# A new deal of the eight PSUM banks in a FoX attention layer with a SwiGLU feed-forward

## The chip, the core and the metric

The kernel runs on one core of a Trainium2 chip. The metric is the device time of one execution in microseconds (us); the time of a kernel is the median over its runs.

## What is computed

The input is a sequence of 1024 tokens of width 1024, with 16 learned meta tokens put ahead of it, so 1040 positions. The core computes one layer of forgetting attention with 16 heads of 64, then a SwiGLU feed-forward with 2816 hidden units, then a last RMS norm. Cut to what matters:

```python
hn = rms_norm(h, attn_norm)
q, k, v, gate, f_logit = split(hn @ w_in)        # 16 heads of 64
q, k = rms_norm(q, q_gain), rms_norm(k, k_gain)  # per head
c = cumsum(log_sigmoid(f_logit + b_f))           # per head, along the tokens
s = q @ k.T * 64**-0.5 + c[query] - c[key]
s = where(key_pos <= query_pos, s, -inf)
h = h + (softmax(s) @ v * sigmoid(gate)) @ w_out
hn = rms_norm(h, ffn_norm)
a, u = split(hn @ ffn_w_in)
h = rms_norm(h + (silu(a) * u) @ ffn_w_out, final_norm)[16:]
```

## The kernel before

All of it is one function. Large products are made of two reduced-precision halves of each operand (`h` and `l` at the end of a name), so that each product takes three matmuls: high by high, high by low, low by high. A half is made by a cast on ACT, and the other by a subtraction on DVE.

**Attention** works on pairs of heads, numbered 0 to 7. A pass over one pair is written as a string of steps: `steady` at L575, `before` at L576 for the pass before the last, `final` at L577. The string interleaves the attention of pair p with the preparation of pair p+1, in program order. The steps and their lines:

- `P0` to `P8`: nine projection tiles `pj_0` to `pj_8` (bank taken in `proj_unit`, matmuls L189 to L195, 16 for `pj_0` and 24 for each other). Tile 0 holds the last 16 tokens. It is evacuated by a copy on ACT (`last`, L204) and an addition on DVE (L205); the others by ACT (L209, L211) and DVE (L212, L220).
- `N`: the norms of q and k. `T`: the transposes `ptk`, `ptq` and `ptl` (L318, L337) into PSUM. Each is split into halves by ACT (L301, L304) and DVE (L302, L305) to `tk`, `tq` and `tl`, and these are put into place by DMA.
- `G`: the two gate tiles `pg_0` and `pg_1` (L445 to L447, 24 matmuls each, evacuated on DVE at L452).
- `S`: the scores of one head and one half of the queries. Each tile `S_e_j` (head e of the pair, key block j) takes two matmuls (L356, L357) and is evacuated to `sb` by ACT (L363); then POOL applies the causal mask (L368) and DVE takes the running maximum `rm` (L374, L378).
- `M`: that maximum transposed by PE (`pm`, L387), reduced by DVE, and spread by PE (`pb`, L392). `X`: subtraction on DVE (L398) and exponential on ACT (L399).
- `O`: scores times values (`O`, L410), copied out by ACT (`o`, L412). `Z`: the sums over keys (`Z`, L431). `L` and `C`: the gate is loaded and combined. `W`: the weights of the pair after the next are loaded and split (ACT L96, DVE L98).
- `A`, in the last pass alone: the output projection (L504 to L506), which accumulates into four tiles `acca` at a time (taken in `acc_tile`, L512), and later `accb`.

**The feed-forward's first product** is a seven-product scheme (Strassen-Winograd) for each of 22 hidden tiles. Each of the seven is a function call `prod` (L718), 12 matmuls into one bank named `f`. Before them the normed rows are transposed by `put` (L648; matmuls L656, split by ACT L659 and DVE L660), which takes its banks by turns from S, S, M, O. For the first three hidden tiles two products each are placed early in the program by `ffn1_early` (L730), between the transposes and the rest. **The second product** accumulates into four banks at a time (`banks`, L906).

**PSUM** has eight banks, and every tile above takes one whole bank. They are dealt in four groups by tag. In a group, each new tile of the program takes the bank that comes free first, and waits until the tile that was in it has been read:

```python
BANKS = {'m': 4, 'S': 2, 'M': 1, 'O': 1}
def bank(tag, name):
    return ps.tile([P, 512], F32, tag=tag, name=name, bufs=BANKS[tag])
```

Group m serves `pj`, `ptk`, `ptq`, `ptl`, `pg`, `acc` and `f`; group S the score tiles; group M `pm`, `pb` and `Z`; group O the tile `O`.

**The order on each engine** isn't the order of the program. A scheduler simulates the program on a time line of its own and gives every engine a fixed list; an instruction that would wait for a bank in that simulation is placed later, behind others that are ready. On the chip each engine works through its list in order: a waiting instruction holds up all that stand behind it.

Of the kernel before, what the change touches and what calls it, by code (L numbers as in the profile page):

```python
# [30 lines left out]
def f32v(ap):  # L31
    return ap.bitcast(F32)
# [3 lines left out]
def fox_block(ctx, tc, hT, hN, wqkvg, w0f, w0g, wo, w1, w2, g_attn, g_ffn, g_fin, g_q, g_k, b_f, out):  # L36
# [38 lines left out]
    sm = ctx.enter_context(tc.tile_pool(name="sm", bufs=1))  # L75
    ps = ctx.enter_context(tc.tile_pool(name="ps", bufs=2, space=PS))

    BANKS = {'m': 4, 'S': 2, 'M': 1, 'O': 1}

    def bank(tag, name):  # L80
        return ps.tile([P, 512], F32, tag=tag, name=name, bufs=BANKS[tag])

# [394 lines left out]
    def oproj(hf):  # L477

        cs = slice(512 * hf, 512 * hf + 512)
        ob = big.tile([P, NK, D], F32R, tag=("xh", "xl")[hf], name=f"ob{hf}")  # L480

        def raw_tile(name, src):
            raw = wp.tile([P, 512], F32, tag="wraw", name=name, bufs=3)
            nc.sync.dma_start(raw, src)
            return raw

        def stage_o(k):
            raw = state[k]["o", hf][0] if k == NK - 1 else raw_tile(f"ogr{hf}_{k}", ogd[k, :, cs])
            nc.scalar.copy(ob[:, k, :512], raw)
            nc.vector.tensor_tensor(ob[:, k, 512:1024], raw, f32v(ob[:, k, :512]), ALU.subtract)  # L490

        def stage_wo(dc, k):
            raw = raw_tile(f"wor{hf}_{dc}_{k}", wo[k][:, 512 * dc : 512 * dc + 512])
            hi = wp.tile([P, 512], F32R, tag="wh", name=f"woh{hf}_{dc}_{k}", bufs=8)
            lo = wp.tile([P, 512], F32R, tag="wl", name=f"wol{hf}_{dc}_{k}", bufs=8)
            nc.scalar.copy(hi, raw)
            nc.vector.tensor_tensor(lo, raw, f32v(hi), ALU.subtract)
            return hi, lo

        def mm(acc, i, k, w, whole=False):  # L500
            first = k == 0 or (k == NK - 1 and not whole)
            last = k == NK - 1 or (k == NK - 2 and not whole)
            oh, ol = ob[:, k, i * P : (i + 1) * P], ob[:, k, 512 + i * P : 512 + (i + 1) * P]
            nc.tensor.matmul(acc, lhsT=oh, rhs=w[0], start=first, stop=False)  # L504
            nc.tensor.matmul(acc, lhsT=oh, rhs=w[1], start=False, stop=False)
            last_mm[0] = nc.tensor.matmul(acc, lhsT=ol, rhs=w[0], start=False, stop=last)  # L506

        def add(dc, i, acc, src):
            ds_ = slice(512 * dc, 512 * dc + 512)
            nc.vector.tensor_tensor(h1[4 * hf + i][:, ds_], acc, src[:, ds_], ALU.add)  # L510

        def acc_tile(n, dc, i):  # L512
            return bank("m", f"acc{n}{hf}_{dc}_{i}")

        for dc in range(2 - hf):
            accs = [acc_tile("a", dc, i) for i in range(4)]
            for k in range(NK - 1):
                if dc == 0:
                    stage_o(k)
                w = stage_wo(dc, k)  # L520
                for i in range(4):
                    mm(accs[i], i, k, w, hf == 1)
                if k + 2 < NK:
                    yield
            if dc == 0:
                for i in range(4 * hf, 4 * hf + 4):
                    h1.append(ap_.tile([P, D], F32, tag="QQQQVVKK"[i], name=f"h1_{i}", bufs=4 if i < 4 else 2))
                    nc.sync.dma_start(h1[i], hN[META + i * P : META + (i + 1) * P, :])
            if hf == 0:
                for i in range(4):  # L530
                    add(dc, i, accs[i], h1[i])
            yield
        stage_o(NK - 1)
        if hf == 1:
            w = stage_wo(0, NK - 1)
            for i in range(4):
                mm(accs[i], i, NK - 1, w, True)
                add(0, i, accs[i], h1[4 + i])
            w = [stage_wo(1, k) for k in range(NK)]
        else:  # L540
            w = [stage_wo(dc, NK - 1) for dc in range(2)]
        for i in range(4):
            for dc in range(hf, 2):
                acc = acc_tile("b", dc, i)
                for k in range(NK) if hf == 1 else (NK - 1,):
                    mm(acc, i, k, w[k] if hf == 1 else w[dc], hf == 1)
                add(dc, i, acc, h1[4 * hf + i])
            nc.sync.dma_start(hd[4 * hf + i], h1[4 * hf + i])
            yield i
# [7 lines left out]
    gate0 = [[t[:, k * P : (k + 1) * P] for k in range(NK)] for t in (g0h, g0l)]  # L557
    proj_begin(0)
    n0 = 7
    pjs = [bank("mmmmSSM"[j], f"pj0_{j}") for j in range(n0)]  # L560
    for k in range(NK):
        for j in range(n0):
            proj_mm(0, j, k, pjs[j])
# [15 lines left out]
    for p in range(-1, NK):  # L579
        for op, *a in (first if p < 0 else steady if p + 2 < NK else before if p + 1 < NK else final).split():  # L580
            a = [int(x) for x in a]
# [129 lines left out]
    def split(src, name):  # L711
# [3 lines left out]
        nc.vector.tensor_tensor(lo, src, f32v(hi), ALU.subtract)  # L715
        return hi, lo

    def prod(t, n, s, op):  # L718
        pp = bank("m", f"f{n}_{t}")
        for k in range(4):  # L720
            ks = slice(k * P, (k + 1) * P)
            bh, bl = RB[op](k)
            nc.tensor.matmul(pp, lhsT=s[0][:, ks], rhs=bh, start=(k == 0), stop=False)  # L723
            nc.tensor.matmul(pp, lhsT=s[0][:, ks], rhs=bl, start=False, stop=False)  # L724
            nc.tensor.matmul(pp, lhsT=s[1][:, ks], rhs=bh, start=False, stop=(k == 3))  # L725
        return pp
# [3 lines left out]
    def ffn1_early(t):  # L730

        x1, c11 = (t512("cmb", f"wa{t}_{c}") for c in range(2))
        for c, r in enumerate((x1, c11)):
            nc.sync.dma_start(r, w1[t, 0, :, 512 * c : 512 * c + 512])
        p1 = prod(t, 1, split(x1, f"a11_{t}"), "b11")
        nc.scalar.copy(x1, p1)
        p2 = prod(t, 2, split(c11, f"a12_{t}"), "b21")
        tt(c11, p2, x1, ALU.add)
        return x1, c11
# [10 lines left out]
    def ffn1(t, raw, early):  # L750
# [10 lines left out]
        if early is None:  # L761
            p1 = prod(t, 1, w, "b11")
            x1 = t512("cmb", f"x1_{t}")
            nc.scalar.copy(x1, p1)
        else:
            x1, c11 = early
# [137 lines left out]
    nprod = [0]  # L904

    def banks(name):  # L906
        nprod[0] += 1
        tags = ("SSMO", "mmmm")[nprod[0] % 2]
        return [bank(g, f"y{name}_{n}") for n, g in enumerate(tags)]

    def left(name, h):
# [10 lines left out]
    def prod2(name, n, blocks, upto=NHP, ahead=None, after=None):  # L922
        py = banks(n)
        for h in range(upto):
            g = left(name, h)
            if ahead is not None:
                ahead(h)
            w = split(blocks[h], f"w{n}_{h}")
            for i in range(4):
                mm(py[i], i, h, g, w)  # L930
            if after is not None:
                after(h)
        return py
# [165 lines left out]
```

## Time and profile before

| | |
|---|---|
| median of 3 runs | 1472.07 us (1471.94 to 1474.59) |
| the profiled execution | 1471.29 us, span 1469.6 us |
| PE busy in the span | 1395.4 us, 95% |
| DVE, ACT, POOL busy | 1032.4 us (70%), 675.3 us (46%), 453.2 us (31%) |
| mean granted TensorE clock | 0.979 of full speed |
| matmuls | 6699 |

PE is the engine that runs matmuls, PEld its loading of weights, DVE the vector engine, ACT the scalar engine, POOL the general engine, SP the one that issues DMAs. A row of a timeline gives the start, the duration, the engine and line, what was written from what, and in brackets how long the engine stood idle before it and whose work ended that. A number such as 0.50 under PEclk is the TensorE clock granted in that stretch, as a share of full speed (2.4 GHz), so 0.50 is the lower level, 1.2 GHz. The profiled execution took 1.7 us more than the span, which lies around it. Matmuls overlap each other, so the time from start to start says what one costs.

### The profile page before, as it was taken

What the parts mean: (1) busy time and instruction counts of PE and PEld (TensorE: products, weight loads), DVE (VectorE), ACT (ScalarE), POOL (GpSimd) and SP (SyncE); (2) the same over time, 40 slices, a digit from 0 to 9 for tenths busy, and PEclk for the clock granted to TensorE, in tenths of its full rate; (3) what the DMA queues carried; (4) which work ended last, traced back from release to release, by engine and by line L of the source; (5) the groups of instructions that cost most, each with busy time, mean ns of one, the idle gap of its engine ahead of it and who ended that gap; (6) DMA issues with size and microseconds to landing.
All of it is one profiled execution on the core that took longest, in us unless ns stands there. A gap on an engine that the chain in (4) does not pass through costs nothing. (4 is left out here: it accounts for less than half of the span.)

```text
span 1469.6 us, 20413 instructions
## 1 busy us (share of the span) xinstructions
PE 1395.4 (95%) x6699; PEld 1123.5 (76%) x6699; DVE 1032.4 (70%) x1819; ACT 675.3 (46%) x1444; POOL 453.2 (31%) x532
## 2 busy tenths in 40 slices
PE   7999898999999898999799999999999999999996
PEld 7897777878878777756468788888888888876874
DVE  7647566757757666667887786666666666799696
ACT  6445445555555545555654433223332323434535
POOL 4002524324252525334224011111111111496082
PEclk9999999999999999999899999999999999999998
DMA  6334234250614233175463233333323227653343
GB/s 197 108 98 133 73 95 114 52 165 23 168 46 133 72 109 97 30 176 181 170 229 115 100 108 108 107 108 107 107 94 107 89 91 271 233 171 98 94 143 144
DMA packets 103197, 178.86 MB, mean 122 GB/s; under 512 B 16553, under 2 KB 25778, under 8 KB 103090
## 3 DMA queue, kind: packets, MB, share of 16 engines
q1 hardware_dynamic: 103090, 177.55, 38.9%
q8 instruction: 53, 0.87, 0.2%
q14 instruction: 54, 0.44, 0.1%
HBM read 109.46 MB, written 38.54 MB: 101 GB/s over the span
## 5 line engine op out<-in xcount | busy, mean ns | idle before, releaser
L193 PE MATMUL pj<-wh,xhb 128*128 128x384 f32 (+1 forms) x512 | 181.2, 355 | 15.6 <-DVE last L205 10.2
L368 POOL TENSOR_SCALAR_AFFINE_SELECT sb<-sb 128x128 f32<-128x128 f32 (+2 forms) x160 | 60.4, 380 | 431.5 <-ACT sb L363 430.8
L194 PE MATMUL pj<-wl,xhb 128*128 128x384 f32 (+1 forms) x512 | 179.5, 351 | 0.0
L195 PE MATMUL pj<-wh,xlb 128*128 128x384 f32 (+1 forms) x512 | 177.2, 350 | 0.0
L363 ACT ACTIVATE sb<-S,nb 128x512 f32<-128x512 f32 (+4 forms) x224 | 118.2, 537 | 126.2 <-PE S L357 124.3
L422 POOL TENSOR_TENSOR t<-t,sb 128x512 f32<-128x512 f32 (+4 forms) x160 | 139.5, 898 | 0.0
L802 POOL TENSOR_TENSOR gs<-u,u 128x512 f32<-128x512 f32 x11 | 14.2, 1287 | 380.4 <-DVE u L789 380.4
L193 PEld LDWEIGHTS pj<-wh,xhb 128*128 128x128 f32 x512 | 100.4, 196 | 20.2 <-DVE last L205 11.5
L378 DVE TENSOR_TENSOR rm<-rm,sb 128x512 f32<-128x512 f32 (+4 forms) x160 | 85.1, 532 | 38.1 <-POOL sb L368 18.1
L398 DVE TENSOR_TENSOR sb<-sb,pb 128x512 f32<-128x512 f32 (+4 forms) x224 | 95.7, 496 | 21.8 <-PE pb L392 21.8
L194 PEld LDWEIGHTS pj<-wl,xhb 128*128 128x128 f32 x512 | 100.6, 196 | 4.1 <-issue 2.4
L195 PEld LDWEIGHTS pj<-wh,xlb 128*128 128x128 f32 x512 | 100.1, 196 | 3.8 <-issue 2.4
L399 ACT ACTIVATE sb<-sb 128x512 f32<-128x512 f32 (+4 forms) x224 | 93.6, 476 | 11.7 <-DVE sb L398 8.3
L410 PE MATMUL O<-sb,V 128*64 128x512 f32 (+4 forms) x448 | 94.4, 471 | 2.9 <-ACT sb L399 2.9
L356 PE MATMUL S<-Q,K 128*128 128x512 f32 (+4 forms) x224 | 80.8, 361 | 16.2 <-ACT sb L363 16.2
L357 PE MATMUL S<-Q,K 128*128 128x512 f32 (+4 forms) x224 | 72.3, 325 | 0.8 <-DMA Q<-tq 0.8
L356 PEld LDWEIGHTS S<-Q,K 128*128 128x128 f32 (+1 forms) x224 | 39.0, 174 | 44.0 <-ACT sb L363 28.0
L410 PEld LDWEIGHTS O<-sb,V 128*64 128x64 f32 (+1 forms) x448 | 35.4, 137 | 42.4 <-issue 22.2
L769 DVE TENSOR_TENSOR u<-f,x 128x512 f32<-128x512 f32 x19 | 13.1, 692 | 64.7 <-PE f L725 64.6
L96 ACT CAST wh<-wraw 128x512 fp32r<-128x512 f32 (+1 forms) x64 | 38.2, 606 | 40.1 <-DMA wraw<-wqkvg 31.6
L374 DVE TENSOR_TENSOR rm<-sb,sb 128x400 f32<-128x400 f32 (+1 forms) x32 | 20.5, 642 | 49.6 <-ACT sb L363 49.5
L98 DVE TENSOR_TENSOR wl<-wraw,wh 128x512 fp32r<-128x512 f32 x56 | 40.1, 736 | 12.2 <-ACT wh L96 12.2
(1374 smaller groups left out, 3940.6 us busy)
## 6 DMA issues: line engine op xcount, KB each, us to landing
Q<-tq SPq DMA_DIRECT2D x128, 128.0 KB, 2.3
wraw<-wqkvg SPq DMA_DIRECT2D x56, 256.0 KB, 3.6
av<-w SPq DMA_DIRECT2D x22, 512.0 KB, 3.2
gs<-qs SPq DMA_DIRECT2D x44, 256.0 KB, 2.6
ga<-qa SPq DMA_DIRECT2D x33, 256.0 KB, 2.9
K<-tk SPq DMA_DIRECT2D x64, 128.0 KB, 2.4
wor<-wo SPq DMA_DIRECT2D x32, 256.0 KB, 3.0
a11r<-w SPq DMA_DIRECT2D x22, 256.0 KB, 3.2
```

The lines of the kernel that those rows point to most:

```text
L193: nc.tensor.matmul(o, lhsT=xh[k][:, sl], rhs=wh, start=(k == 0), stop=False)
L194: nc.tensor.matmul(o, lhsT=xh[k][:, sl], rhs=wl, start=False, stop=False)
L195: last_mm[0] = nc.tensor.matmul(o, lhsT=xl[k][:, sl], rhs=wh, start=False, stop=(k == NK - 1))
L356: nc.tensor.matmul(psx[:n, s0:], lhsT=kk[:, j * P : j * P + n], rhs=q[:, 0, s0:], start=True, stop=False)
L357: nc.tensor.matmul(psx[:n, s0:], lhsT=kk[:, j * P : j * P + n], rhs=q[:, 1, s0:], start=False, stop=True)
L363: nc.scalar.activation(sj, psx[:n, s:], AF.Identity, bias=nbias[c][:n, j, head : head + 1], scale=1.0)
L368: nc.gpsimd.affine_select(out=sj[:, : t_end - s], in_=sj[:, : t_end - s], compare_op=ALU.is_ge, fill=NEG, base=b + s - j * P, pattern=[[1, ...
L378: nc.vector.tensor_tensor(rm[:n, s:], rm[:n, s:], sj, ALU.max)
L398: nc.vector.tensor_tensor(sj, sj, mx[:n, s:], ALU.subtract)
L399: nc.scalar.activation(sj, sj, AF.Exp, bias=0.0, scale=1.0)
L410: nc.tensor.matmul(po[r, s:], lhsT=st["V"][:n, j, r], rhs=sj, start=(i == 0), stop=(i == nt - 1))
L422: nc.gpsimd.tensor_tensor(total[e][:n, s:], src[:n, s:], sj, ALU.add)
```

## The change

Group m gives one bank to group S. The fourth of the tiles `acca` and one of the first seven `pj` of the start move to S with it. The `f` tiles of the first feed-forward product are no longer all in group m: a counter takes them through all eight banks. The second product's groups of four are made up anew. No operation is added or taken away; lines behind L717 stand three further down.

```diff
-    BANKS = {'m': 4, 'S': 2, 'M': 1, 'O': 1}
+    BANKS = {'m': 3, 'S': 3, 'M': 1, 'O': 1}
...
         def acc_tile(n, dc, i):
-            return bank("m", f"acc{n}{hf}_{dc}_{i}")
+            return bank("mmmS"[i] if n == "a" else "m", f"acc{n}{hf}_{dc}_{i}")
...
-    pjs = [bank("mmmmSSM"[j], f"pj0_{j}") for j in range(n0)]
+    pjs = [bank("mmmSSSM"[j], f"pj0_{j}") for j in range(n0)]
...
+    nprod1 = [0]
+
     def prod(t, n, s, op):
-        pp = bank("m", f"f{n}_{t}")
+        nprod1[0] += 1
+        pp = bank("mSMmSOmS"[nprod1[0] % 8], f"f{n}_{t}")
...
     def banks(name):
         nprod[0] += 1
-        tags = ("SSMO", "mmmm")[nprod[0] % 2]
+        tags = ("SSSO", "mmmM")[nprod[0] % 2]
```

What this does to the scheduler's lists is seen in three places. In the names, the first numbers are the tile's own, as above, and the last is a running number that tells tiles of different passes apart.

**The end of the third pass (pair 2), on PE.** Before, the last product `O_1` is followed at once by score tiles of the next pair and then by a projection:

```order
L410 MATMUL O_1_3523<-sb_1_8_3214,V_1862 64x16
L356 MATMUL S_0_1_3680<-Q_1_0_3370,K_1_3342 128x400
L357 MATMUL S_0_1_3680<-Q_1_0_3370,K_1_3342 128x400
L356 MATMUL S_0_2_3688<-Q_1_0_3370,K_1_3342 128x272
L357 MATMUL S_0_2_3688<-Q_1_0_3370,K_1_3342 128x272
L193 MATMUL pj_4_3948<-wh_0_3564,xhb 128x384
```

Now transposes, a projection's beginning and the smaller score tiles of the other half stand there:

```order
L410 MATMUL O_1_3523<-sb_1_8_3214,V_1862 64x16
L318 MATMUL ptq_1_3623<-ident,raw_2_2789 128x128 x2
L318 MATMUL ptq_1_3623<-ident,raw_3_2790 128x128 x2
L189 MATMUL pj_0_3725<-wh_0_3564,xtail 128x256
L190 MATMUL pj_0_3725<-wl_0_3565,xtail 128x256
L189 MATMUL pj_0_3725<-wh_1_3570,xtail 128x256
L356 MATMUL S_0_3_3444<-Q_0_0_3365,K_0_3341 128x256
L357 MATMUL S_0_3_3444<-Q_0_0_3365,K_0_3341 128x256
L356 MATMUL S_0_4_3452<-Q_0_0_3365,K_0_3341 16x16
```

The score tiles that stood right behind `O_1` moved later, and `pj_4` with them.

**The same place on ACT.** Before, the copy of `O_1` stands ahead of the two evacuations of score tiles:

```order
L412 COPY o_1_3542<-O_1_3523 128x512
L363 ACTIVATE sb_0_0_3423<-S_0_0_3420,nb_253 128x512
L363 ACTIVATE sb_0_0_3675<-S_0_0_3672,nb_253 128x512
L460 ACTIVATE Ga_1_3644<-cg_1_3642 128x512
L204 COPY last_3742<-pj_0_3725 16x256
```

Now:

```order
L363 ACTIVATE sb_0_1_3431<-S_0_1_3428,nb_253 128x400
L363 ACTIVATE sb_0_2_3439<-S_0_2_3436,nb_253 128x272
L96 CAST wh_5_3594<-wraw_5_3592 128x512
L412 COPY o_1_3542<-O_1_3523 128x512
L301 ACTIVATE tq_1_0_3628<-ptq_1_3623,gqk 128x512
L363 ACTIVATE sb_0_3_3447<-S_0_3_3444,nb_253 128x144
L363 ACTIVATE sb_0_4_3455<-S_0_4_3452,nb_253 16x16
L96 CAST wh_6_3600<-wraw_6_3598 128x512
L363 ACTIVATE sb_0_0_3423<-S_0_0_3420,nb_253 128x512
L96 CAST wh_7_3606<-wraw_7_3604 128x512
```

Two evacuations moved ahead of the copy, and that of `S_0_0` behind it and behind one of three weight casts.

**The gate of the third pass, on PE.** Before, `ptk_0` stands eight rows ahead of this piece, and score and `O` matmuls follow until `pg_0` begins:

```order
L356 MATMUL S_1_7_2994<-Q_0_1_2702,K_0_2411 128x256
L357 MATMUL S_1_7_2994<-Q_0_1_2702,K_0_2411 128x256
L410 MATMUL O_0_3103<-sb_0_0_2745,V_1862 64x512
...
L387 MATMUL pm_0_1_3128<-ident,rm_1_2949 128x128
...
L410 MATMUL O_0_3103<-sb_0_4_2525,V_1862 64x16
L445 MATMUL pg_0_3465<-xhb,wh_0_2634 128x512
```

Now:

```order
L318 MATMUL ptk_0_3343<-ident,raw_0_2787 128x128 x2
L318 MATMUL ptk_0_3343<-ident,raw_1_2788 128x128 x2
L410 MATMUL O_1_3523<-sb_1_0_2953,V_1862 64x512
L431 MATMUL Z_0_3326<-t_0_0_3116,one 64x512
L431 MATMUL Z_0_3326<-t_0_1_3117,one 64x512
L318 MATMUL ptq_0_3356<-ident,raw_0_2787 128x128 x2
L318 MATMUL ptq_0_3356<-ident,raw_1_2788 128x128 x2
L337 MATMUL ptl_3375<-ident,raw_3_2791 128x16
L445 MATMUL pg_0_3465<-xhb,wh_0_2634 128x512
```

Between `ptk_0` and `pg_0` there are now three large matmuls and the small transposes.

**The entry of the feed-forward, on PE.** Before, an early product (`f_11`, hidden tile 11) runs among the transposes:

```order
L725 MATMUL f_11_8930<-b_2_8078,a_11l 128x512
...
L723 MATMUL f_11_8930<-b_3_8079,a_11h 128x512
L724 MATMUL f_11_8930<-b_7_8083,a_11h 128x512
L656 MATMUL ptt_2_8724<-ident,hl_0_8697 128x128 x4
L656 MATMUL ptb_0_8802<-ident,h_4_8436 128x128 x2
L656 MATMUL ptt_2_8731<-ident,t_2_8719 128x128 x4
```

Now the transposes follow each other, and the first early product in a bank that they use comes behind the last of them:

```order
L656 MATMUL ptb_3_8867<-ident,h_7_8442 128x128 x4
L656 MATMUL ptt_3_8851<-ident,t_3_8796 128x128 x4
L656 MATMUL ptt_3_8874<-ident,h_7_8442 128x128 x4
L726 MATMUL f_0_8890<-b_0_8076,a_0h 128x512
L727 MATMUL f_0_8890<-b_4_8080,a_0h 128x512
```

Of the six early products, the two in group m still stand ahead of the transposes, and the other four behind.

## Rows read from the trace of the kernel before

**Rows 1.** Stretches: start:end, length, PE PEld DVE ACT POOL busy, PEclk, DMA, GB/s.

```profile
164.00:247.00 83.00, 79.02 (x421) 64.71 (x421) 55.10 (x115) 44.97 (x104) 29.64 (x47) 0.96 0.36 96
765.00:830.00 65.00, 62.39 (x298) 50.80 (x297) 49.54 (x98) 31.50 (x79) 17.34 (x12) 0.93 0.31 108
830.00:1245.00 415.00, 415.00 (x1785) 335.37 (x1785) 279.01 (x431) 127.48 (x218) 57.44 (x44) 1.00 0.34 115
```

**Rows 2.** The waits of PE: waiter, releaser, us in total, times, longest.

```profile
PE S L356 <- ACT sb L363: 16.2, 22, 2.0
PE pj L193 <- DVE last L205: 10.2, 6, 1.8
PE ptq L318 <- DVE tk L305: 1.9, 1, 1.9
```

**Rows 3.** Timeline, end of the third pass: PE, ACT, DVE; last, PE in the fourth.

```profile
331.18 0.45 PE L356 MATMUL S<-Q,K 128*128 128x400 f32 x1 [1.30 <-ACT sb L363]
333.96 0.69 PE L193 MATMUL pj<-wh,xhb 128*128 128x384 f32 x1 [1.68 <-DVE last L205]
...
329.95 0.58 ACT L412 COPY o<-O 128x512 f32<-128x512 f32 x1 [3.75 <-PE O L410]
330.44 1.27 ACT L363 ACTIVATE sb<-S,nb 128x512 f32<-128x512 f32 x2
332.25 0.36 ACT L204 COPY last<-pj 16x256 f32<-16x256 f32 x1
...
333.49 0.41 DVE L205 TENSOR_TENSOR last<-pj,last 16x256 f32<-16x256 f32 x1
...
412.70 0.45 PE L356 MATMUL S<-Q,K 128*128 128x400 f32 x1 [0.63 <-ACT sb L363]
```

**Rows 4.** Stretches behind the first and the second such place, columns as in rows 1.

```profile
166.40:173.20 6.80, 5.28 (x16) 5.28 (x17) 6.80 (x13) 3.78 (x11) 6.80 (x6) 0.51 0.01 4
251.90:255.30 3.40, 3.40 (x13) 3.40 (x12) 3.40 (x7) 1.98 (x7) 3.40 (x3) 0.50 0.00 0
255.30:258.70 3.40, 3.40 (x23) 3.37 (x22) 2.89 (x9) 0.76 (x3) 3.40 (x4) 1.00 0.12 30
```

**Rows 5.** Timeline of PE in the middle of the feed-forward's first product.

```profile
1005.08 0.39 PE L723 MATMUL f<-bb,s_5h 128*128 128x512 f32 x1
1005.31 0.40 PE L724 MATMUL f<-bb,s_5h 128*128 128x512 f32 x1
```

**Rows 6.** The page's costliest groups: xcount, busy us, mean ns, idle before.

```profile
L96 ACT CAST wh<-wraw 128x512 fp32r<-128x512 f32 (+1 forms) x64 | 38.2, 606 | 40.1 <-DMA wraw<-wqkvg 31.6
```

**Rows 7.** Timeline, PE and DVE: both windows of `ptk` in the third pass, and `Z`.

```profile
281.19 0.60 PE L318 MATMUL ptk<-ident,raw 128*128 128x128 f32 x4
284.87 0.68 DVE L305 TENSOR_TENSOR tk<-ptk,tk 128x512 fp32r<-128x512 f32 x1
299.92 0.60 PE L318 MATMUL ptk<-ident,raw 128*128 128x128 f32 x4
303.70 4.19 DVE L398 TENSOR_TENSOR sb<-sb,pb 128x512 f32<-128x512 f32 x9
309.02 0.67 DVE L305 TENSOR_TENSOR tk<-ptk,tk 128x512 fp32r<-128x512 f32 x1
308.03 1.08 PE L431 MATMUL Z<-t,one 128*64 128x512 f32 x4
```

**Rows 8.** Timeline of PE in the last pass of attention.

```profile
718.92 0.30 PE L387 MATMUL pm<-ident,rm 128*128 128x128 f32 x1 [2.39 <-ACT woh L496]
763.86 0.79 PE L504 MATMUL acca<-woh,ob 128*128 128x512 f32 x1 [2.26 <-ACT ob L489]
```

**Rows 9.** The feed-forward's entry: PE, DVE, and a stretch with the columns of rows 1.

```profile
818.72 0.79 PE L723 MATMUL f<-bb,s_0h 128*128 128x512 f32 x1 [2.19 <-ACT bb L659]
...
818.15 0.68 DVE L715 TENSOR_TENSOR s_0l<-s,s_0h 128x512 fp32r<-128x512 f32 x1
...
818.50:825.30 6.80, 6.17 (x15) 4.41 (x16) 4.60 (x9) 4.99 (x9) 0.00 (x0) 0.50 0.46 154
```

## The prediction

> **What bounds the kernel now.** I first read the busy times by stretch. In the middle of the feed-forward's first product PE is busy for all of 415.00 us at full clock; in the attention's first full pass it lacks four of 83 us and its clock is at 0.96; at the feed-forward's entry it is at 0.93 [rows 1]. So PE's list sets the time, and only its idle pieces and its stretches at the lower clock can be won. Next I read the waits of PE: the two lines that come back in every pass are scores that wait for ACT's evacuation, 16.2 us in 22 waits, and projections that wait for DVE's `last`, 10.2 us in 6 [rows 2]. The timeline of the third pass shows where these two meet. PE ends `O_1`, wants a bank of group S, and stands idle for 1.30 us, because the evacuation that frees it stands on ACT behind the copy of `O_1`, which could only start at 329.95. Then `pj_4` waits 1.68 us more for a bank that `pj_0` holds until DVE has read it, at 333.90; DVE waited for ACT's copy at 332.25, and that stood behind the same evacuations [rows 3]. After this pause the clock falls to 0.50 for 3.40 us, in which 13 matmuls are done, where the next 3.40 us hold 23 [rows 4].
>
> The place comes six times, from 163 to 577 us. Five of the six score waits are of 1.30 as the one shown, one is of 0.63, 7.1 together, and the six projection waits are the whole 10.2 [rows 2, 3]. The clock falls each time: for two such stretches of 3.40 in the first place and for one in each other, so seven stretches [rows 4].
>
> **The change, part by part.** All is set against the profiled execution, 1471.29 us, which lies 0.8 below the median of the runs.
>
> *The feed-forward through eight banks.* Its matmuls already follow each other every 0.23 us [rows 5] without a gap [rows 1]. A bank that comes free earlier has nobody waiting for it: 0. A rule of the Trainium skill speaks for more: "Perfetto Trace Analysis", section "Matmul Optimizations", asks that all eight banks be leveraged. By it the product itself would be faster; by the row it can't be, since four banks leave PE no idle time to give back. The measured row decides, and the rule goes to the rivals.
>
> *End of a pass.* With three S banks the list puts `ptq`, `pj_0` and small scores behind `O_1`. Two score evacuations stand ahead of the copy, so two banks are free when PE arrives, and PE has transposes and a projection to go on with. The two waits and the pause go, and with them the falls of the clock. Gain: 7.1 + 10.2 = 17.3 for the waits, and for each slow stretch ten matmuls of 3.40 / 23 = 0.148, so 1.5, times seven, 10.4 [rows 4]. Together **-27.7**. What is late next is ACT: copy 0.58, one score evacuation of 0.64 (half of the two in [rows 3]) and two casts of 0.61 [rows 6] are 2.4 us until the bank of `S_0_0` is free. Some 26 projection matmuls stand on PE ahead of the next tile that needs it, at 0.148 each 3.8 us, so I take this as covered; without that cover the 1.30 is back, and with the pause the clock's fall (second rival).
>
> *The gate of each pass.* This is the new wait. With three m banks `pg_0` takes the bank of `ptk_0`, and must wait for `tk` on DVE. Before, the low half ended at 285.55, which is 3.76 after `ptk` had ended at 281.79, and eight rows of other work lay between [rows 7]. Now one `O` matmul, two of `Z` and the `ptq` transposes do: about 0.5, 1.0 and 0.5, some 2 us by [rows 7] (`Z` 1.08 in all, `ptk` 0.60). So the wait is 1.8 if the split takes as long as it did there, and 0 if ACT and DVE take it up at once. I take 1.4, near the first end: the same two queues are as full, and the one case in which something waited for such a split cost 1.9 [rows 2]. Seven gated passes: +10 (0 to 13). Where that pause is longest the clock may fall too; two of seven at 1.5: **+13** in all. `pg_1` takes `ptq`'s bank, but 21 matmuls of `pg_0` stand ahead of it, 4.9 us by the pitch of [rows 5]: 0. Behind the waiting `pg_0` on PE stands `pm` of the next half; it is not due earlier than it was.
>
> *The other score waits* are 16.2 - 7.1 = 9.1 in 16. A third bank lets PE run one tile further ahead of ACT. It takes between none and all; where ACT itself is the slower it only puts the wait off, so I take a third: **-3** (0 to -9).
>
> *The last pass.* `acca`'s fourth tile takes a bank of S, so its 21 matmuls are moved between the scores and `pm`, or to the end. They are 4.9 us of work without a wait of their own. The wait ahead of `pm`, 2.39 with smaller ones behind it, and the one ahead of `acca` at 763.86, 2.26 [rows 8], can be filled. I take 3 for the first place, and 2 and a slow stretch's 1.5 for the last: **-6.5** (0 to -8).
>
> *The feed-forward's entry.* Of the six early products four now stand behind the transposes. Their 48 matmuls, 11.2 us at 0.233 [rows 5], no longer lie between transposes that wait for ACT and DVE. In exchange some nine DVE operations of 0.68 [rows 9], which made these products' operands and read them, are no longer in the transposes' way: 6.1 won back. That leaves **+5** (0 to +11). What was lost there before, a wait of 2.19 and a stretch of 6.8 us with 15 matmuls [rows 9], stays in one form or another.
>
> *The start* has three banks instead of four for the first transposes and the gate: **+1** (0 to +3). The second product's banks only change owners between groups of four: 0.
>
> Sum: -27.7 + 13 - 3 - 6.5 + 5 + 1 = -18.2, so **1453.1 us**.
>
> **The rivals.** *The gate becomes the bound (slower).* The third pass's second window shows a split that ended at 309.69, 9.2 after its `ptk` at 300.52 [rows 7]. If `tk` stands as late for the gate, each pass waits 9.2 - 2 = 7.2, 50 in all instead of 10, and all seven clocks fall, 10.4 instead of 3: +48, so 1501. It decides from about 3.3 a pass: to end 2.9 above the time before, 21.1 must be lost again; five more falls of the clock are 7.5 of it, and the rest is 1.9 a pass on top of my 1.4. For it: DVE's list decides, and DVE is the second busiest [rows 1]. Against it: ahead of that split DVE had the exponentials' nine subtractions to do, 4.19 us in one piece [rows 7]; in the changed list only small maxima and evacuations stand there. Chance 0.11. The skill has a rule that speaks for this case: "TensorE: Matmul & The Clock Gate", section "A second HAM failure mode: psum-queue depth-cycling", tells of a kernel in which cycling through PSUM banks left small idle pieces between groups of matmuls, and the clock swung. The trace agrees that small pieces are enough, with 1.30 and 1.68 ahead of a fall [rows 3, 4]; that dealing banks in turn makes them, no row shows.
>
> *The stop at the end of a pass is only displaced (slower).* The freeing of `S_0_0`'s bank stands behind the copy of `O_1` and two weight casts, and a cast waits for its DMA. If that lands late, PE stands at the next scores as it did before, and the clock falls as before. Then the -27.7 are gone and the rest stays: 1480.8. It decides once the evacuation is more than 3.8 us behind PE's arrival. Against it: the casts before came without being waited for at this place. Chance 0.10.
>
> *The gate's wait is hidden (faster still).* If the split is taken up at once, the 13 go: 1440. Chance 0.14.
>
> *All eight banks make the first product itself faster.* Then what could be won is what the stretch ahead of the middle lacks, 65.00 - 62.39 = 2.6 of idle time and about 3.3 of slow clock (29 matmuls of 0.233 fit in 6.8, 15 were done [rows 1, 9]), and my +5 falls away: about 1442. Chance 0.02.
>
> *Most of it cancels.* The list changes as shown but half of the gain at the end of a pass is lost to the same clock at the gate: 1467 to 1474. Chance 0.07.
>
> **How the numbers follow.** The forecast's chance is 0.56, with its own range from 1444 to 1465. A measurement of this kernel can tell some 0.2% from no change, 2.9 us. Faster by more: forecast, hidden gate and eight banks, 0.56 + 0.14 + 0.02 = 0.72. Within it: 0.07. Slower: 0.11 + 0.10 = 0.21. The range takes in the hidden gate with the other terms' better ends, down to 1434, and the cancelled and part of the displaced case up to 1478; it leaves out the long gate and some of the displaced stop, 0.2 together.
>
> **What would show it.** Right: no wait of PE for `last` (L205) at the end of a pass, score waits of 6 us or so in all, at most two or three stretches at 0.50 in the attention, a wait of `pg` (L445) for `tk` of 1 to 2 us in seven places, and the middle of the first product at its 0.23 as before. Wrong: waits of `pg` of more than 4, a score wait behind the casts at each pass's end, or an entry of the feed-forward that is longer by more than 11.

## The result, and the profile after

The changed kernel took 1450.01 us (median of four runs, 1445.11 to 1452.52), the kernel before 1473.33 beside it: a ratio of 0.9835, with a 95% interval from 0.9803 to 0.9866. The forecast was 1453.1, with a range from 1434 to 1478. The profiled execution took 1449.52 us against 1471.29, 21.8 less.

The sum was nearly right, and several of its terms were not. What follows is about both.

The head of the page, with the busy times of the engines:

```profile
span 1447.9 us, 20369 instructions
PE 1381.0 (95%) x6699; PEld 1115.0 (77%) x6699; DVE 1041.0 (72%) x1819; ACT 679.2 (47%) x1444; POOL 448.4 (31%) x532
```

The stretches that answer to [rows 1], with the same columns:

```profile
164.00:247.00 83.00, 80.98 (x455) 66.49 (x454) 60.09 (x128) 49.01 (x115) 34.76 (x58) 1.00 0.34 98
765.00:830.00 65.00, 58.12 (x277) 46.66 (x275) 51.58 (x92) 28.60 (x61) 12.94 (x8) 0.97 0.27 93
830.00:1245.00 415.00, 415.00 (x1788) 336.22 (x1787) 276.61 (x420) 131.45 (x224) 65.54 (x49) 1.00 0.36 126
```

Between 164 and 247 us, in the attention, PE does 455 matmuls where it did 421, and the clock is at 1.00 instead of 0.96. In the middle of the feed-forward's first product nothing changed: 415.00 of 415.00 busy, 1788 matmuls and 1785 before. (The middle row is not the same work as in [rows 1]: the kernel is some 20 us further there.)

The waits of PE, to be laid beside [rows 2]:

```profile
PE acca L505 <- DVE wol L497: 7.3, 2, 6.8
...
PE pm L387 <- DVE rm L376: 5.7, 5, 2.0
PE accb L504 <- DVE h L510: 5.0, 2, 3.5
PE pj L190 <- DVE wl L98: 5.0, 2, 2.6
...
PE S L356 <- ACT sb L363: 0.6, 2, 0.4
```

Scores waited 16.2 us and now wait 0.6; the line of `last` (10.2 in 6) is gone. No line of `pg` has appeared. Grown are waits for what DVE makes: `wol` and `wl` (the low halves of weights), 0.2 and 0.3 us in the kernel before, `rm` (the running maximum), of which only L378 was waited for (2.7, now 2.2), and the addition `h` at L510, which was not waited for.

The end of the third pass. PE, then ACT:

```profile
303.72 0.86 PE L410 MATMUL O<-sb,V 128*64 128x272 f32 x7
304.51 0.66 PE L318 MATMUL ptq<-ident,raw 128*128 128x128 f32 x4
304.92 0.36 PE L189 MATMUL pj<-wh,xtail 128*128 128x256 f32 x1
...
304.74 0.59 ACT L412 COPY o<-O 128x512 f32<-128x512 f32 x1
305.21 0.71 ACT L301 ACTIVATE tq<-ptq,gqk 128x512 fp32r<-128x512 f32 x1
```

PE goes from `O_1` into the transposes and a projection without a bracket, so without idle time, while ACT makes the copy. That is the pause of [rows 3] gone. And with it the clock: of the seven slow stretches that lay behind the six places, none is left between 85 and 630 us.

To see where the 21.4 us between the two lists of matmuls lie, I gave each matmul the time that its shape usually takes from start to start in the kernel before (1310.0 us in all, the same for both kernels). What a kernel takes beyond that is its loss, and the losses can be compared over the same amount of work, also where the order differs:

| PE's work, us | place | loss before | loss after | difference | forecast |
|---|---|---|---|---|---|
| 0 to 80 | start | 12.6 | 14.7 | +2.1 | +1 |
| 80 to 530 | six passes | 72.8 | 46.1 | -26.7 | -17.7 |
| 530 to 640 | last passes | 28.2 | 31.2 | +3.0 | -6.5 |
| 640 to 740 | feed-forward's entry | 12.7 | 12.9 | +0.2 | +5 |
| 740 to the end | both products | 13.6 | 13.6 | 0.0 | 0 |

The six passes gave more than forecast and the last passes less; these errors nearly cancelled.

The usual times decide to which row a loss at a boundary goes, so the table is firm in its sum and less so in its rows: with other usual times from the same trace the six passes come to between -24 and -31, and the rows of the last passes and the entry move against each other. Two places need no usual times, because both kernels have done the same matmuls there, shape by shape: after 3893 and after 4025 matmuls, on either side of the first product's beginning. PE, first in the kernel before, then in the changed one:

```profile
798.99 0.39 PE L724 MATMUL f<-b,a_0h 128*128 128x512 f32 x1
828.90 0.40 PE L723 MATMUL f<-bc,s_0h 128*128 128x512 f32 x1
```

```profile
773.59 0.48 PE L727 MATMUL f<-b,a_1h 128*128 128x512 f32 x1
807.40 0.39 PE L728 MATMUL f<-bb,s_0l 128*128 128x512 f32 x1
```

The changed kernel is 25.4 us ahead at the first and 21.5 at the second, and 21.5 it stays. So the entry cost 3.9 and not 0.2: in the table, the wait of 2.26 at 763.86 [rows 8] and the slow clock behind it, which belong to the last pass of the kernel before, fall into the entry's row. By the same count the changed kernel is 1.9 behind after 351 matmuls (79.58 against 77.68), and 28.6 ahead after 3271 (618.78 against 647.41), just before the output projection begins in both. So the passes up to there gave 30.5, and the last pass lost 3.2.

### The profile page after: what moved, and what is told of

Read it like the earlier page. It is cut to its first block, busy times and chain, and to the rows that moved or that the text cites. A ratio compares the mean times of both kernels' runs of the same rounds, so it can differ in the third digit from the quotient of the medians.

```text
span 1447.9 us, 20369 instructions
## 1 busy us (share of the span) xinstructions
PE 1381.0 (95%) x6699; PEld 1115.0 (77%) x6699; DVE 1041.0 (72%) x1819; ACT 679.2 (47%) x1444; POOL 448.4 (31%) x532
## 4 chain that ended last, share of the span: by engine, by line
PE 72%; DVE 13%; DMA 7%; issue 4%; ACT 2%; SPq 1%; POOL 0%; DVEq 0%; ACTq 0%; POOLq 0%
PE f L726 10%; PE f L728 10%; PE f L727 10%; PE pj L193 5%; PE pj L194 5%; PE pj L195 5%; DMA wraw<-wqkvg 5%; PE O L410 3%; PE y L922 2%; PE y L923 2%; PE y L921 2%; PE S L356 2%; PE S L357 2%; PE pg L445 1%; PE pg L446 1%
## 5 line engine op out<-in xcount | busy, mean ns | idle before, releaser
L193 PE MATMUL pj<-wh,xhb 128*128 128x384 f32 (+1 forms) x512 | 176.2, 346 | 7.2 <-ACT xhb L139 5.9
L194 PE MATMUL pj<-wl,xhb 128*128 128x384 f32 (+1 forms) x512 | 175.7, 343 | 0.0
L195 PE MATMUL pj<-wh,xlb 128*128 128x384 f32 (+1 forms) x512 | 172.5, 341 | 0.0
L399 ACT ACTIVATE sb<-sb 128x512 f32<-128x512 f32 (+4 forms) x224 | 94.1, 478 | 40.7 <-DVE sb L398 40.6
L193 PEld LDWEIGHTS pj<-wh,xhb 128*128 128x128 f32 x512 | 97.5, 191 | 11.4 <-ACT xhb L139 6.4
L378 DVE TENSOR_TENSOR rm<-rm,sb 128x512 f32<-128x512 f32 (+4 forms) x160 | 87.0, 544 | 20.4 <-ACT sb L363 8.6
L194 PEld LDWEIGHTS pj<-wl,xhb 128*128 128x128 f32 x512 | 97.7, 191 | 4.2 <-issue 2.4
L195 PEld LDWEIGHTS pj<-wh,xlb 128*128 128x128 f32 x512 | 97.1, 190 | 1.5
L356 PE MATMUL S<-Q,K 128*128 128x512 f32 (+4 forms) x224 | 76.2, 344 | 0.7 <-ACT sb L363 0.6
L357 PE MATMUL S<-Q,K 128*128 128x512 f32 (+4 forms) x224 | 71.3, 323 | 0.0
L98 DVE TENSOR_TENSOR wl<-wraw,wh 128x512 fp32r<-128x512 f32 x56 | 48.9, 884 | 30.7 <-ACT wh L96 30.3
L374 DVE TENSOR_TENSOR rm<-sb,sb 128x400 f32<-128x400 f32 (+1 forms) x32 | 36.8, 1150 | 24.4 <-ACT sb L363 21.3
```

What stands on the lines that cost most here:

```text
L193: nc.tensor.matmul(o, lhsT=xh[k][:, sl], rhs=wh, start=(k == 0), stop=False)
L194: nc.tensor.matmul(o, lhsT=xh[k][:, sl], rhs=wl, start=False, stop=False)
L195: last_mm[0] = nc.tensor.matmul(o, lhsT=xl[k][:, sl], rhs=wh, start=False, stop=(k == NK - 1))
L356: nc.tensor.matmul(psx[:n, s0:], lhsT=kk[:, j * P : j * P + n], rhs=q[:, 0, s0:], start=True, stop=False)
L357: nc.tensor.matmul(psx[:n, s0:], lhsT=kk[:, j * P : j * P + n], rhs=q[:, 1, s0:], start=False, stop=True)
```

## The experiments

The theory after the result: the gain is the third bank of group S, the turn of the `f` tiles through eight banks is a loss if anything, and what now holds PE up is DVE standing still beside POOL. Every run is compared with the kernel before on the same chip.

**One part of the change alone: the attention's banks.**

```diff
-        pp = bank("mSMmSOmS"[nprod1[0] % 8], f"f{n}_{t}")
+        pp = bank("m", f"f{n}_{t}")
```

> Three S and three m banks as in the change, but the feed-forward's first products all in group m as before. Theory (the gain is the end of each attention pass: score waits, waits for `last`, and the clock's falls behind them): the six passes are those of the changed kernel, so 1446 to 1455 us; score waits of PE under 2 us, none for `last`; the middle of the first product stays at 0.233 us a matmul with three banks. Rival (the products' eight banks carry part of the gain): 1460 or more, and idle time of PE inside the first product.

Measured: 1445.64 us, ratio 0.9814 (0.9785 to 0.9843). All of the gain is there without the eight banks. With three banks instead of eight the first product is as dense as before:

```profile
830.00:1245.00 415.00, 415.00 (x1789) 335.89 (x1788) 276.17 (x417) 133.31 (x227) 67.63 (x51) 1.00 0.37 127
```

The score waits are 2.3 us in 4, a little over the 2 expected.

**The other part alone: the products' turn through the banks, on the kernel before.**

> The banks stay dealt as before (four m, two S), and only the first products go through all groups in turn. Theory: the attention's seven slow-clock stretches and the 16.2 + 10.2 us of waits stay, the first product gains nothing, and the entry of the feed-forward costs up to 5 more: 1468 to 1479 us. Rival (eight banks help the product): 1462 or less.

Measured: 1475.7 us, ratio 1.0013 (1.0000 to 1.0026). No gain. Its waits in the attention are the ones of before:

```profile
PE S L356 <- ACT sb L363: 16.9, 24, 1.7
PE pj L193 <- DVE last L205: 10.2, 6, 1.8
```

By the account of losses its entry into the feed-forward (640 to 740 of the work) lost 17.2, against 12.7 before. In e1 that piece lost 7.0, in the changed kernel 12.9. So the turn costs some 4.5 to 5.9 us there. Counted by the same matmuls, e1 is 23.4 us ahead of the kernel before after 3893 and 25.8 after 4025: the attention's banks alone win 2.4 there, and this is how the changed kernel comes out with 3.9.

**The early products alone back in group m.**

```diff
-        pp = bank("mSMmSOmS"[nprod1[0] % 8], f"f{n}_{t}")
+        pp = bank("m" if nprod1[0] <= 6 else "mSMmSOmS"[nprod1[0] % 8], f"f{n}_{t}")
```

> The changed kernel, but the six early products all in group m, the later ones through all banks. By the prediction's entry term they stand among the transposes again and win back 5 us: 1445. By the changed kernel's trace, in which the entry lost nothing in all, 1447 to 1453.

Measured: 1456.25 us, ratio 0.9864 (0.9829 to 0.9899), above both expectations. The entry did get better, to a loss of 9.8. But two passes of the attention, which this edit doesn't touch in the source, lost 10.3 and 13.0 where the changed kernel lost 7.1 and 8.1. In the second of them PE waits 6.3 us at once for `rm`; I come back to that wait. This run can't tell the term by its total.

**One bank further: two m, four S.**

```diff
-    BANKS = {'m': 3, 'S': 3, 'M': 1, 'O': 1}
+    BANKS = {'m': 2, 'S': 4, 'M': 1, 'O': 1}
...
-            return bank("mmmS"[i] if n == "a" else "m", f"acc{n}{hf}_{dc}_{i}")
+            return bank("mmSS"[i] if n == "a" else "m", f"acc{n}{hf}_{dc}_{i}")
...
-    pjs = [bank("mmmSSSM"[j], f"pj0_{j}") for j in range(n0)]
+    pjs = [bank("mmSSSSM"[j], f"pj0_{j}") for j in range(n0)]
...
-        tags = ("SSSO", "mmmM")[nprod[0] % 2]
+        tags = ("SSSS", "mmMO")[nprod[0] % 2]
```

> The change taken one bank further: two m banks, four S banks (the output projection's four tiles in m, m, S, S; the second product's groups remade). Theory: score waits are down to 0.6 us in the changed kernel, so a fourth S bank wins under 1 us; two m banks make each projection wait for the evacuation of the one before the last, and the two gate tiles for both transposes' splits, 2 to 5 us a pass with falls of the clock: 1465 to 1490. Rival (more S banks still gain, m banks are plentiful): 1450 or less.

Measured: 1514.43 us, ratio 1.0269 (1.0229 to 1.0309): the direction was right, the size too small. Here PE waits again and again for the transposes' splits (`tk` and `tq`, 19.1 us in the three lines below `wl`); the largest line, though, is the low half of a weight, `wl`:

```profile
PE pj L190 <- DVE wl L98: 27.9, 6, 8.5
PE pj L189 <- DVE tk L305: 7.7, 7, 2.4
...
PE pj L193 <- DVE tq L302: 6.2, 7, 1.6
PE ptl L337 <- DVE tk L305: 5.2, 8, 0.7
```

**The bank given to group M instead of S.**

```diff
-    BANKS = {'m': 3, 'S': 3, 'M': 1, 'O': 1}
+    BANKS = {'m': 3, 'S': 2, 'M': 2, 'O': 1}
...
-    pjs = [bank("mmmSSSM"[j], f"pj0_{j}") for j in range(n0)]
+    pjs = [bank("mmmSSMM"[j], f"pj0_{j}") for j in range(n0)]
...
-        tags = ("SSSO", "mmmM")[nprod[0] % 2]
+        tags = ("SSMO", "mmmM")[nprod[0] % 2]
```

> As e1_attn_only, but the bank that group m gives up goes to group M (pm, pb, Z) instead of S: three m, two S, two M. Theory (the gain needs the third S bank): score waits stay near 16 us, the waits for `last` and some seven slow-clock stretches stay too, 1465 to 1485. Rival (any other deal makes the scheduler's list better, and S is not the point): 1455 or less.

Measured: 1483.73 us, ratio 1.0063 (1.0043 to 1.0083). The same bank taken from m gains nothing here; only as a third S bank does it make a gain. What this run loses against the kernel before it loses late: after 3305 matmuls it is 3.2 us behind, after 3751, with most of the output projection done, 17.3. There the fourth of the tiles `acca` takes one of only two S banks; that this is the cause is not shown. The pattern of before is all there, with ten stretches of 3.4 us at 0.50 behind the six places:

```profile
PE S L356 <- ACT sb L363: 14.4, 17, 1.3
PE pj L193 <- DVE last L205: 10.6, 6, 1.8
```

**What holds PE up now.** The largest single wait of the changed kernel is in the last pass. PE, DVE and POOL there, in that order:

```profile
636.32 0.80 PE L505 MATMUL acca<-wol,ob 128*128 128x512 f32 x1 [6.85 <-DVE wol L497]
...
626.85 8.27 DVE L374 TENSOR_TENSOR rm<-sb,sb 128x400 f32<-128x400 f32 x1
635.22 0.44 DVE L378 TENSOR_TENSOR rm<-rm,sb 128x272 f32<-128x272 f32 x1
635.58 0.69 DVE L497 TENSOR_TENSOR wol<-wor,woh 128x512 fp32r<-128x512 f32 x1
...
626.33 0.72 POOL L368 TENSOR_SCALAR_AFFINE_SELECT sb<-sb 128x112 f32<-128x112 f32 x1
627.03 7.65 POOL L422 TENSOR_TENSOR t<-t,sb 128x512 f32<-128x512 f32 x7
```

One maximum of two score tiles runs for 8.27 us on DVE, and ends when POOL's chain of seven additions has ended (627.03 + 7.65 = 634.68). `wol`, for which PE waits, stands behind it in DVE's list. All executions of that operation (L374), shortest, median and longest in ns, first in the kernel before, then in the changed one:

```profile
L374 DVE TENSOR_TENSOR rm<-sb,sb x32: 555/686/717, 84.2 to 704.1; 128x400 f32<-128x400 f32 x16, 128x512 f32<-128x512 f32 x16
```

```profile
L374 DVE TENSOR_TENSOR rm<-sb,sb x32: 555/743/8270, 82.6 to 680.2; 128x400 f32<-128x400 f32 x16, 128x512 f32<-128x512 f32 x16
```

The same amount of data, so the 8.27 is no work. The Trainium skill names such a thing ("SBUF — State Buffer", section "SBUF: two separate sides"): a DVE operation with two inputs in SBUF and a POOL operation that reads SBUF share a pair of ports, the one that starts first has it for its whole instruction, and the other stands. The row agrees as far as DVE stood; that it stood for a whole chain of seven, and not for one instruction, is more than the page says.

The wait inside the passes is of the same kind. At the end of the third pass, DVE and then POOL:

```profile
311.41 3.22 DVE L98 TENSOR_TENSOR wl<-wraw,wh 128x512 fp32r<-128x512 f32 x1
...
311.60 2.48 POOL L422 TENSOR_TENSOR t<-t,sb 128x512 f32<-128x512 f32 x2
```

A subtraction of 0.69 takes 3.22, and `pj_0` waits for it for 2.44 us (312.25 to 314.69). If standing beside POOL is the cause, less work on POOL at these places should help, although it comes on top of a DVE that is busier than POOL.

**The additions before the last pass on DVE.** In `attn_out`, for pair 6 and the second half of the queries (the same computation on another engine):

```diff
-                nc.gpsimd.tensor_tensor(total[e][:n, s:], src[:n, s:], sj, ALU.add)
+                eng.tensor_tensor(total[e][:n, s:], src[:n, s:], sj, ALU.add)
...
+            eng = nc.vector if (p, c) == (NK - 2, 1) else nc.gpsimd
```

> As e1_attn_only, but the 16 additions of the sums over keys (L422) of the last pair but one, second half, run on DVE instead of POOL. Theory (in the last pass a two-input DVE operation stands still beside POOL's chain of additions: 8.27 us at 626.85 in the changed kernel where such a one takes 0.64, and PE waits 6.8 for what is queued behind it): that wait goes, the 16 additions cost DVE some 8 us of its own, 1 to 7 us faster than e1: 1439 to 1445. Rival (DVE is simply full there): the wait stays or grows, 1446 to 1454.

Measured: 1447.58 us, ratio 0.9810 (0.9759 to 0.9862), no different from e1, and as a time in the rival's range. The rival's sign is not there, though: the wait of 6.8 for `wol` is gone, the longest L374 takes 1.67, and the piece from 530 to 590 of the work lost 9.6 instead of 14.5, as the theory had it. But two passes further up now each had this on DVE, with chains of POOL beside it, and lost 12.8 and 13.7. In the second of them PE waits 6.27 us at once for `rm`, and the clock is at 0.50 behind it (DVE, PE, and a stretch with the columns of [rows 1]):

```profile
475.37 9.84 DVE L378 TENSOR_TENSOR rm<-rm,sb 128x272 f32<-128x272 f32 x3
...
485.38 1.11 PE L387 MATMUL pm<-ident,rm 128*128 128x128 f32 x4 [6.27 <-DVE rm L376]
...
487.70:491.10 3.40, 3.40 (x13) 3.40 (x11) 0.81 (x2) 0.26 (x1) 1.47 (x3) 0.50 0.08 19
```

In e1 and e3 one pass had such a group of maxima, here and in e8 two, in the changed kernel none. Which passes fall into it changes with edits elsewhere; why it strikes one pass and not the next stays open.

**Half of the additions on DVE in every pass.** The same edit with the condition `(c, e) == (1, 1)`.

> As e1_attn_only, but in every pass the additions of the second head, second half of the queries, run on DVE instead of POOL (64 additions, some 30 us more for DVE in all). Theory of the stand-still beside POOL: POOL's chains at the end of the passes are half as long, single DVE operations over 1.5 us become rare, and the waits for `rm` and `wl` (9 to 11 us in e1 and the changed kernel) shrink: 1435 to 1446. Rival (DVE's own load decides): 1447 to 1465.

Measured: 1439.77 us, ratio 0.9766 (0.9727 to 0.9805). The time is in the theory's range, though the interval overlaps e1's, and DVE has 64 additions more without being the limit. But one of the theory's signs failed. The waits for `rm` were to shrink and grew, first in e1, then here:

```profile
PE pm L387 <- DVE rm L376: 9.1, 4, 5.4
```

```profile
PE pm L387 <- DVE rm L376: 14.7, 7, 2.8
```

The longest is half as long, and there are more of them. By the count of same matmuls this run is still 2.0 us behind e1 after 3251 matmuls, before the output projection begins, and 5.2 ahead after 3893: what it wins, it wins in the last pass, where the waits for `wol` and for `h` have gone.

**All additions of the second head on DVE**, with the condition `e == 1`.

> As e7, but the second head's additions of both halves run on DVE (96 additions). If POOL's chains still hold DVE up elsewhere: 1432 to 1439. If DVE's own load is now the limit: 1441 to 1455.

Measured: 1434.29 us, ratio 0.9717 (0.9678 to 0.9756), the fastest of all, 1.2 points below the changed kernel's ratio. The longest execution of the operation from above takes 1.66 us, about what it takes in e6 and e7, where it took 8.27 in the changed kernel; in the six passes PE waits 7.9 us for `rm` and `wl`, against 10.7 in the changed kernel:

```profile
L374 DVE TENSOR_TENSOR rm<-sb,sb x32: 551/670/1658, 83.9 to 667.0; 128x400 f32<-128x400 f32 x16, 128x512 f32<-128x512 f32 x16
```

The six passes (80 to 530) lost 40.7 in it, 46.1 in the changed kernel and 47.8 in e1. This run's interval lies below e1's without overlap.

**The same edit of e7 on the banks of before, and on the changed kernel.**

> The kernel before with e7's edit alone (additions of the second head, second half of the queries, on DVE), banks dealt as before. Theory (POOL's chain holds DVE up where it matters only once PE no longer stops at the end of a pass): the score waits, the waits for `last` and the slow clock stay, and the edit is worth under 6 us: 1468 to 1478. Rival (the chains on POOL cost the same under either deal): 1462 to 1467 or less.

Measured: 1461.73 us, ratio 0.9902 (0.9870 to 0.9933). The theory missed this one: it allowed 6 us and the edit brought about 14 by the ratio (the two traced executions differ by 8.9). What it said of the six passes holds. The slow stretches stay, and the waits move from one line to the other instead of going, 25.0 us against 26.4:

```profile
PE pj L193 <- DVE last L205: 21.3, 6, 3.8
...
PE S L356 <- ACT sb L363: 3.7, 8, 1.3
```

The six passes lost 69.1 instead of 72.8. More of the gain came from the last passes and the entry together (36.0 instead of 40.9), as the rival has it: POOL's chains cost something under either deal.

> The changed kernel with e7's edit. If the first products' eight banks cost the 4 to 6 us at the feed-forward's entry that e1 and the changed kernel differ by there, this lies as much above e7: 1443 to 1447. If that difference was chance: 1437 to 1442.

Measured: 1443.8 us, ratio 0.9793 (0.9745 to 0.9841). It lost 11.8 at the entry (640 to 740), e7 5.1. With e1 against the changed kernel (7.0 and 12.9) and the kernel before against e2 (12.7 and 17.2) that makes three pairs with the same sign and 4.5 to 6.7 us each (4.5 to 6.8 by the count of same matmuls). The intervals of the totals overlap in e1's and e7's pairs, so it is the piece of the trace, not the totals, that shows it.

**A try at the waits of `accb`**, with tags from m and S by turns for these tiles:

```diff
-            return bank("mmmS"[i] if n == "a" else "m", f"acc{n}{hf}_{dc}_{i}")
+            return bank("mmmS"[i] if n == "a" else "mSmS"[i], f"acc{n}{hf}_{dc}_{i}")
```

> As e1_attn_only, but the output projection's later tiles `accb` take their banks from m and S by turns instead of m alone. If the waits of `accb` for DVE's addition (5.1 us in 2) are for a bank, they go: 1440 to 1446. If they come from DVE's place in the list, no change: 1444 to 1449.

Measured: 1462.72 us, ratio 0.9931 (0.9909 to 0.9953), above both expectations. The waits of `accb` left the list, so they were for a bank; but the feed-forward's transposes take S banks at the same time, and their list was remade so that they wait for POOL:

```profile
PE ptt L656 <- POOL hl L694: 12.6, 3, 6.1
```

## Why the prediction was right, and where it wasn't

*The end of a pass (-27.7)* was right: both waits and all seven slow stretches went, and e5, without the third S bank, has both again. The waits that went are 7.1 + 10.2; the clock's share stays the price of ten matmuls in each stretch, since no run changed the clock alone.

*The gate (+13)* is the step that failed. With three m banks `pg_0` comes right behind the three transposes, as forecast, but no wait appeared. I carried the split's delay of 3.76 us over from the list before [rows 7]. The changed list in the third pass, PE and then DVE:

```profile
281.19 0.60 PE L318 MATMUL ptk<-ident,raw 128*128 128x128 f32 x4
...
284.16 0.23 PE L337 MATMUL ptl<-ident,raw 16*128 16x16 f32 x1
284.32 0.50 PE L445 MATMUL pg<-xhb,wh 128*128 128x512 f32 x1
...
283.49 0.67 DVE L305 TENSOR_TENSOR tk<-ptk,tk 128x512 fp32r<-128x512 f32 x1
```

The low half ends at 284.16, 2.38 after `ptk`, and `pg` begins at 284.32. The delay is 1.77 to 2.71 in the seven gated passes, and the work between is 2.53 here where I had 2.0. The gate's own rival (0.11) was the further off; "the wait is hidden" (0.14) was the mechanism that came, though not with its time of 1440. Scarce m banks do cost what the step was about once there are only two: 19.1 us of such waits in e4.

*The other score waits (-3)*: all but 0.6 of 9.1 went, -8.5. Of this 4.8 lay in the six passes and the rest behind them.

*What the forecast did not have* are the new waits for `rm` and `wl`, 10.7 us in the six passes. So these passes come to -27.7 - 4.8 + 10.7 = -21.8, against the -26.7 of the account. Of the difference, 1.5 are waits of `O` for ACT's exponentials (L399) that went too; for some 3 us I have no cause.

*The last pass (-6.5)* came out at +3.0 (3.2 by the count). The two waits that it names went, and others came: 5.0 us for DVE's addition `h`, ahead of `accb`, and the one for `wol`. Filling the waits with `acca` was thought of as free work; PE then reached weights whose low half DVE had not made, because an operation of DVE ahead of it ran for 8.27 us beside POOL's chain: 6.85 us, and the clock at 0.52 behind it:

```profile
638.20:641.60 3.40, 3.40 (x13) 2.65 (x12) 2.31 (x4) 1.11 (x2) 1.51 (x2) 0.52 0.85 316
```

e6 took POOL's chain away from that place, and the wait with it.

*The entry (+5)* was the right price of the change in the products, 4.5 to 6.7 in three pairs. In the total it came out at 3.9, since the attention's banks won 2.4 there, which the forecast didn't have.

*The feed-forward through eight banks (0)* was right in e1, e2 and after. The rule of the Trainium skill on using all eight banks ("Perfetto Trace Analysis", section "Matmul Optimizations") gave nothing here: PE is busy for 415.00 of 415.00 us with four banks, with three and with eight.

*The small pauses and the clock.* Of what the Trainium skill tells of cycling through banks ("TensorE: Matmul & The Clock Gate", section "A second HAM failure mode: psum-queue depth-cycling") the runs show nothing: in the product that goes round all eight the clock is 1.00. A single pause lowered it in some places and not in others. Behind those of 6.85 (above) and 6.27 (e6) it is at 0.52 and 0.50; `pj_0`'s wait of 2.44 in the changed kernel is followed by stretches at full clock:

```profile
313.40:316.80 3.40, 2.11 (x13) 2.09 (x14) 3.18 (x6) 2.71 (x5) 2.16 (x3) 1.00 0.82 212
316.80:320.20 3.40, 3.40 (x23) 3.40 (x22) 3.37 (x8) 1.54 (x5) 3.40 (x4) 1.00 0.23 84
```

*The sum.* That the total came within 3.1 us of the measured median is in good part luck. The gate's 13 did not come and the score waits gave 5.5 more than taken; new waits of 10.7 and a last pass nearly 10 worse than forecast took that back.

## What to carry to other kernels

Give a bank to the group whose tiles wait behind another engine's queue, and not to the product that already runs without gaps; a pause can cost the slow clock behind it beside its own length, so look first for pauses that come back in every pass. A split's delay or a queue's delay belongs to its list: when the order changes, count anew what stands ahead of it on each engine. When PE's waits go, ask which engine it meets next, and look there for single operations that are many times their median.

## What was not expected of the hardware

A DVE operation with two inputs in SBUF can stand still for a whole chain of POOL operations: 8.27 us beside seven additions of 7.65, where the same operation takes 0.56 to 0.72 in the kernel before, and 1.67 at most once that chain is taken from POOL (e6). The shared ports are the Trainium skill's reason ("SBUF — State Buffer", section "SBUF: two separate sides"); the runs show the two engines' times alone. Moving additions from POOL (448 us busy) to DVE (1041 us busy) made the kernel faster, by about half a point of the ratio for each step on e1 (0.9814, 0.9766, 0.9717 for none, 64 and 96 additions moved), though the intervals of neighbouring steps overlap, and by one point on the banks of before. Only the longest stand-stills went with it: the waits for `rm` grew in e7.
